# A two-layer hybrid decoder trunk: other buffer counts, joined attention scores, values in three chunks, a re-arranged end

## The chip, the cores and the metric

The kernel runs on one core of a Trainium2 chip. The metric is the device time of one execution in microseconds, as the median of several runs. The core has a matrix engine (TensorE, PE in the profile; PEld is its weight load), three engines for elementwise work (VectorE, DVE; ScalarE, ACT; GpSimd, POOL), and queues that start DMA transfers, most of them on SyncE (SP). Matmul results land in PSUM, which has eight banks of 512 float32 per partition; all else lives in SBUF.

## The reference

256 tokens of width 1024 go through two layers in float32. Cut to what matters:

```
x += 0.5 * SwiGLU_1(rms(x))                      # D_FF = 2816
h  = rms(x) @ W_in -> [rx | rgate | q | k | v | f_logit | gA | gB]
ya = (RG_LRU(conv4(rx)) * gelu(rgate)) @ w_rnn_out
# 8 heads of 128: q, k RMS-normalised
s  = q k^T / sqrt(128) + dcum[query] - dcum[key]   # dcum = cumsum(log_sigmoid(f_logit + f_b))
yb = (softmax(causal s) v) @ w_attn_out            # in query blocks of 128
x += (sigmoid(gA) * ya + sigmoid(gB) * yb) @ W_o
x += 0.5 * SwiGLU_2(rms(x))
x += sigmoid(rms(x) @ W_pg + b_pg) * (p @ W_pe)
# after both layers: final RMSNorm, output (1, 256, 1024)
```

## The kernel before

Activations stand transposed (features on partitions, tokens along the row) nearly everywhere. Every float32 factor is split into a high part, rounded to the matmul's own float32 format, and a low remainder, and a product is three matmuls: high by high, high by low, low by high (`mm3`, `mm3m`, L306 to L314; `mm2`, L344, does the first two as one 512-column matmul against the activation's high and low halves side by side).

**Weights** (`Weights`, L49 to L116) stream through SBUF in the order of a plan (L159 to L174). One entry of the plan is one DMA, mostly 1 MB, into a *raw* buffer (tag `wr`, three of them). It is cut into two *units*; of each, ScalarE writes the high part (L95) and VectorE the remainder (L96), into unit buffers (tags `wh` and `wl`, five of each). `next` (L110) hands a unit to the matmuls and emits the work for those up to four ahead. A raw buffer comes free when its second unit is split, a unit buffer when the matmuls that read it are done. `apart` (L98) loads one more 1 MB piece through a raw buffer into buffers of its own: the recurrent gates' weights in the first feed-forward's down projection of each layer, the embedding's in that of the second, both behind output tile 2 (L502). The down projection (L486 to L503) takes four units for each of its eight output tiles; an output tile's first matmul is that of L347.

**At the start**, four tiles `hd` hold input and first weights together (L181 to L189). They use the tag `wr` too, so that the fourth waits until the first has been used. `load_first` (L62) then loads the next two entries of the plan.

**Values** (L582 to L608): values and forget logits, 1032 columns, come in four chunks of 258. A chunk has two units of four 128-row blocks each, and for each of two token tiles and eight blocks three matmuls of 258 columns. `gates` (recurrent gates) follow the second, third and fourth chunk.

**Attention** goes head by head in four steps, spread over slots between the matmuls of other projections (`attend`, L753). `step_a` (L690) transposes q and k, splits them and makes a tile `b` (L705) that adds the forget terms in `step_b`. `step_b` (L707) makes the scores of query block 0 against 128 keys (four matmuls of 128 columns) and of block 1 against 256 keys (four of 256 columns) in one PSUM bank, and then for each block minimum (signs are turned), exponential and row sum, and scales the probabilities by the reciprocal on VectorE (L724). `step_c` (L728) transposes them on TensorE (L732), `step_d` multiplies by the values.

**The end** (L915 to L995): the last layer's gate product is made with tokens on partitions. Token tile 1's second half of the features is made in two halves of 256 columns (L990), both in one bank. `finish` (L939) reads the bank (L943), applies tanh (L944), forms the output (L945, L947), squares and sums it (L949) and multiplies by the final gain (L950). `scaled` (L952) forms the mean square (L955, L957), its power -1/2 on GpSimd (L959), and scales: 512 columns on ScalarE (L963), 512 on VectorE (L965), each followed by its output DMA (L966).

The order of instructions on each engine's queue is not the program's own: a planner that simulates the engines at build time sets it from the dependences, and inserts the waits. A dependence on a PSUM tile counts for the tile as a whole.

Of the kernel before, what the change touches and what calls it, by code (L numbers as in the profile page):

```python
# [16 lines left out]
P = 128  # L17
DEPTH = 2
D = 1024
# [21 lines left out]
VC = 258  # L41
# [78 lines left out]
def trunk(ctx: ExitStack, tc: tile.TileContext, head, xT, pT, vec, w1i, w1o, wf, wqk, wv, wg, wro, wao, wo, w2i, w2o,  # L120
# [85 lines left out]
    acol = cp.tile([P, NH], F32, name="acol")  # L206
    mcol = cp.tile([P, NH], F32, name="mcol")
    grp = cp.tile([P, 4], F32, name="grp")
    sel = cp.tile([P, 3], F32, name="sel")
# [27 lines left out]
    def constants():  # L237
        G.memset(mask, 0.0)
        G.affine_select(out=mask[:, P:], in_=mask[:, P:], pattern=[[-1, P]], compare_op=ALU.is_ge, fill=BIG,
                        base=0, channel_multiplier=1)  # L240
        trif = work(s="trif")
        G.memset(trif, 1.0)
        G.affine_select(out=trif[:, :P], in_=trif[:, :P], pattern=[[1, P]], compare_op=ALU.is_ge, fill=0.0,
                        base=0, channel_multiplier=-1)
        G.memset(lfh.bitcast(F32), 0.0)
        G.memset(lfl.bitcast(F32), 0.0)
        for t in rxp:
            G.memset(t[:, 0:3], 0.0)
        V.tensor_copy(out=tri, in_=trif)
        yield  # L250
        V.tensor_tensor(out=acol, in0=ident[:, 0:NH], in1=ident[:, 32:32 + NH], op=ALU.add)
        V.tensor_tensor(out=mcol, in0=ident[:, 64:64 + NH], in1=ident[:, 96:96 + NH], op=ALU.add)
        V.tensor_scalar(out=mcol, in0=mcol, scalar1=-1.0, scalar2=None, op0=ALU.mult)
        yield
        for g in range(4):
            V.tensor_reduce(out=grp[:, g:g + 1], in_=ident[:, 32 * g:32 * g + 32], axis=AX.X, op=ALU.add)
        yield
        V.tensor_tensor(out=sel[:, 0:1], in0=grp[:, 1:2], in1=grp[:, 3:4], op=ALU.add)
        V.tensor_scalar(out=sel[:, 0:1], in0=sel[:, 0:1], scalar1=-1.0, scalar2=None, op0=ALU.mult)
        V.tensor_tensor(out=sel[:, 1:2], in0=grp[:, 0:1], in1=grp[:, 1:2], op=ALU.add)  # L260
        V.tensor_tensor(out=sel[:, 2:3], in0=grp[:, 2:3], in1=grp[:, 3:4], op=ALU.add)
# [244 lines left out]
    def mix(l, n, wgp):  # L506
# [74 lines left out]

        Vh = big([P, TT, 4 * VC], F32R, "vh")  # L582
        Vl = big([P, TT, 4 * VC], F32R, "vl")
        z = kp.tile([P, TT * NH], F32, name=nm("z"), tag="z", bufs=1)
        for c in range(4):
            banks = [two[t]("v") for t in range(TT)]
            for w in range(2):
                wh, wl = W.next()
                for t in range(TT):
                    for i in range(4):  # L590
                        k = 4 * w + i
                        q = slice(i * VC, (i + 1) * VC)
                        mm3m(banks[t][:, 0:VC], a.hi(k, slice(t * P, (t + 1) * P)), a.lo(k, slice(t * P, (t + 1) * P)),
                             wh[:, q], wl[:, q], k == 0, k == KT - 1)
                if w == 0:
                    tick(2)
            for t in range(TT):
# [5 lines left out]
                if c == 3:  # L603
# [7 lines left out]
        dc = kp.tile([P, S], F32R, name=nm("dc"), tag="dc", bufs=1)  # L611
        dk = kp.tile([P, S], F32R, name=nm("dk"), tag="dk", bufs=1)

        def forget():
# [4 lines left out]
            for t in range(TT):  # L619
                oh = lfh[:, t].rearrange("p (g c) -> p g c", g=4)[:, :, 0:NH]  # L620
                ol = lfl[:, t].rearrange("p (g c) -> p g c", g=4)[:, :, 0:NH]
                V.tensor_copy(out=oh, in_=lf3[:, t].to_broadcast([P, 4, NH]))
                V.tensor_tensor(out=ol, in0=lf3[:, t].to_broadcast([P, 4, NH]), in1=oh.bitcast(F32), op=ALU.subtract)
# [9 lines left out]
            V.scalar_tensor_tensor(out=dc, in0=dh.bitcast(F32), scalar=sel[:, 0:1], in1=dps[:, 0:S], op0=ALU.mult,  # L633
                                   op1=ALU.add)
            V.tensor_scalar(out=dk, in0=dc.bitcast(F32), scalar1=sel[:, 1:2], scalar2=sel[:, 2:3], op0=ALU.mult,
                            op1=ALU.add)
# [53 lines left out]
        def step_a(h):  # L690
# [6 lines left out]
            s["q"] = qh, ql = awork(S, "aq", 5), awork(S, "aq", 5)  # L697
            s["k"] = kh, kl = awork(S, "aq", 5), awork(S, "aq", 5)
            s["b"] = awork(S, "aq", 5)
# [5 lines left out]
            A.activation(out=s["b"], in_=dc.bitcast(F32), func=AF.Identity, scale=mcol[:, h:h + 1], bias=acol[:, h:h + 1])  # L705

        def step_b(h):  # L707
            s = st[h]
            (qh, ql), (kh, kl), bl = s["q"], s["k"], s["b"]
# [7 lines left out]
            for t, o, nk in ((0, 0, P), (1, P, S)):  # L717
                V.tensor_tensor_reduce(out=sv[:, o:o + nk], in0=ps[:, o:o + nk], in1=mask[:, S - nk:S], scale=1.0,
# [220 lines left out]
    def finish(t, c, ps, pj, i):  # L939
# [10 lines left out]
        V.tensor_tensor(out=o, in0=o, in1=fgb[:, c], op=ALU.mult)  # L950

    def scaled(t, prior, i):  # L952
# [6 lines left out]
        G.tensor_tensor(out=r, in0=ms, in1=mhalf[:, 0:1], op=ALU.pow)  # L959
        for hf in range(2):  # L960
            o = xo[t][:, hf * 512:(hf + 1) * 512]
            if hf == 0:
                A.activation(out=o, in_=o, func=AF.Copy, scale=r)  # L963
            else:
                V.tensor_scalar(out=o, in0=o, scalar1=r, scalar2=None, op0=ALU.mult)  # L965
# [14 lines left out]
    for t in range(TT):  # L980
        finish(t, slice(0, 512), gp[t], pj[t], t)
    ws = [W.next() for _ in range(4)]
# [4 lines left out]
    pj[1], gp[1] = proj(1, 1), mmbank("gp")  # L987
    finish(0, slice(512, D), gp[0], pj[0], 2)
    scaled(0, [0], 2)
    for i in range(2):  # L990
        c = slice(i * S, (i + 1) * S)
        for u in range(4):
            gate(gp[1][:, c], 1, ws[u], u, c)
        finish(1, slice(512 + c.start, 512 + c.stop), gp[1][:, c], pj[1][:, c], 3 + i)
    scaled(1, [1, 3], 4)  # L995


def _layout(inputs):
# [22 lines left out]
    wv = vf.reshape(L, KT, P, 4, VC).transpose(0, 3, 2, 1, 4).reshape(L, 4, P, KT * VC)  # L1021
# [64 lines left out]
```

## Time and profile before

| | before |
|---|---|
| median of 3 runs, us (lowest to highest) | 1322.03 (1321.92 to 1322.12) |
| profiled execution, us: its time / its span | 1322.07 / 1320.4 |
| mean granted TensorE clock | 0.998 |
| PE busy, us (share of the span), instructions | 1309.2 (99%), 8504 |
| DVE busy | 1072.7 (81%), 2126 |
| ACT busy | 812.8 (62%), 1467 |
| DMA, mean share of 16 engines in the weights' queue | 51.3% |

The busy time of an engine is the union of its instructions' spans. Matmuls are pipelined, so their spans overlap, and what one costs is read from the distance between the starts of two.

### The profile page before, as it was taken

Reading aid. Unit: us, or ns where it says so; the run is one execution under the profiler, and the core shown is the slowest. Engines: PE = TensorE matmul, PEld = TensorE weight load, DVE = VectorE, ACT = ScalarE, POOL = GpSimd, SP = SyncE. Lnnn points to the kernel's source line nnn. Section 1 sums busy time; section 2 is a strip of 40 time slices with the busy share of each in tenths; the row PEclk is TensorE's granted clock in tenths of the full one; section 3 lists DMA queues with packets and bytes.
Section 4 is the critical chain, followed back from the end, with each engine's and each line's share of the span. In section 5 each row is a group of like instructions: output and inputs, shape, how many; then the busy total and the mean of one; then the engine's idle time right before and its main releaser. Section 6 shows DMA issues by size and latency. Waiting matters only on the chain.

```text
span 1320.4 us, 22211 instructions
## 1 busy us (share of the span) xinstructions
PE 1309.2 (99%) x8504; PEld 1191.2 (90%) x8504; DVE 1072.7 (81%) x2126; ACT 812.8 (62%) x1467; POOL 34.4 (3%) x44
## 2 busy tenths in 40 slices
PE   9999999999999999999999999999999999999997
PEld 8888899889999888889988888998899998888896
DVE  7998769899758899876789887698997678998765
ACT  6665656868655666555556656478676556655643
POOL 1000000020000000000000000000200000000000
PEclk9999999999999999999999999999999999999999
DMA  8654665444435555456445546644453455554660
GB/s 294 239 183 157 214 226 193 155 166 172 155 128 191 190 193 191 163 169 243 179 172 192 191 142 219 232 175 160 179 181 128 159 185 198 185 186 155 208 225 33
DMA packets 37258, 241.24 MB, mean 183 GB/s; under 512 B 4128, under 2 KB 4256, under 8 KB 14368
## 3 DMA queue, kind: packets, MB, share of 16 engines
q1 hardware_dynamic: 36864, 239.30, 51.3%
q8 instruction: 67, 1.10, 0.3%
q10 hardware_dynamic: 288, 0.52, 0.1%
q14 instruction: 39, 0.32, 0.1%
HBM read 238.76 MB, written 1.05 MB: 182 GB/s over the span
## 4 chain that ended last, share of the span: by engine, by line
PE 98%; DVE 0%; DMA 0%; ACT 0%; SPq 0%; issue 0%; POOLq 0%
PE mm L350 20%; PE mm L348 11%; PE at L350 11%; PE at L348 6%; PE f L307 3%; PE f L309 3%; PE f L308 3%; PE qk L312 2%; PE qk L314 2%; PE qk L313 2%; PE mm L309 2%; PE mm L307 2%; PE mm L308 2%; PE ya L350 2%; PE mm L347 2%; PE at L347 2%
## 5 line engine op out<-in xcount | busy, mean ns | idle before, releaser
L96 DVE TENSOR_TENSOR wl<-wr,wh 128x1024 fp32r<-128x1024 f32 (+2 forms) x476 | 538.9, 1135 | 147.0 <-ACT wh L95 141.6
L95 ACT ACTIVATE wh<-wr 128x1024 fp32r<-128x1024 f32 (+2 forms) x476 | 467.4, 986 | 307.7 <-PE mm L350 88.3
L350 PE MATMUL mm<-h,wh 128*128 128x512 f32 x616 | 219.3, 394 | 0.0
L350 PE MATMUL at<-h,wh 128*128 128x512 f32 x616 | 218.5, 394 | 0.0
L348 PE MATMUL mm<-h,wl 128*128 128x256 f32 x704 | 182.4, 281 | 0.0
L348 PE MATMUL at<-h,wl 128*128 128x256 f32 x704 | 181.7, 281 | 0.5 <-DVE wl L96 0.5
L350 PE MATMUL mm<-f,wh 128*128 128x512 f32 x504 | 176.8, 394 | 0.0
L348 PE MATMUL mm<-f,wl 128*128 128x256 f32 x528 | 144.1, 280 | 0.0
L348 PEld LDWEIGHTS at<-h,wl 128*128 128x128 f32 x704 | 131.8, 188 | 9.0 <-DVE wl L96 1.0
L348 PEld LDWEIGHTS mm<-h,wl 128*128 128x128 f32 x704 | 131.9, 188 | 7.8 <-DVE wl L96 0.4
L350 PEld LDWEIGHTS mm<-h,wh 128*128 128x128 f32 x616 | 115.7, 188 | 22.5
L350 PEld LDWEIGHTS at<-h,wh 128*128 128x128 f32 x616 | 115.0, 188 | 21.9
L350 PEld LDWEIGHTS mm<-f,wh 128*128 128x128 f32 x504 | 94.5, 188 | 20.7
L307 PE MATMUL f<-h,wh 128*128 128x256 f32 x384 | 108.6, 283 | 0.0
L309 PE MATMUL f<-h,wl 128*128 128x256 f32 x384 | 108.5, 282 | 0.0
L308 PE MATMUL f<-h,wh 128*128 128x256 f32 x384 | 108.4, 282 | 0.0
L348 PEld LDWEIGHTS mm<-f,wl 128*128 128x128 f32 x528 | 99.4, 188 | 2.1
L308 PEld LDWEIGHTS f<-h,wh 128*128 128x128 f32 x384 | 72.4, 189 | 0.1
L307 PEld LDWEIGHTS f<-h,wh 128*128 128x128 f32 x384 | 72.4, 188 | 0.1
L309 PEld LDWEIGHTS f<-h,wl 128*128 128x128 f32 x384 | 72.4, 189 | 0.0
L384 ACT ACTIVATE sum<-mm 128x256 f32<-128x256 f32 x112 | 40.0, 375 | 49.2 <-PE mm L350 49.1
L385 DVE TENSOR_TENSOR sum<-mm,sum 128x256 f32<-128x256 f32 x112 | 45.1, 420 | 14.3 <-ACT sum L384 14.3
(305 smaller groups left out, 2818.0 us busy)
## 6 DMA issues: line engine op xcount, KB each, us to landing
wr<-in_w2i SPq DMA_DIRECT2D x44, 1024.0 KB, 4.8
wr<-in_w1i SPq DMA_DIRECT2D x41, 1024.0 KB, 4.8
wr<-in_wf SPq DMA_DIRECT2D x32, 1024.0 KB, 4.8
wr<-in_w1o SPq DMA_DIRECT2D x32, 704.0 KB, 4.0
wr<-in_w2o SPq DMA_DIRECT2D x32, 704.0 KB, 4.0
wr<-in_wqk SPq DMA_DIRECT2D x16, 1024.0 KB, 4.8
wr<-in_wv SPq DMA_DIRECT2D x8, 1032.0 KB, 5.0
wr<-in_wro SPq DMA_DIRECT2D x8, 1024.0 KB, 4.8
```

The source lines that it names most:

```text
L95: self.nc.scalar.activation(out=hi[:, c], in_=src[:, c], func=AF.Copy)
L96: self.nc.vector.tensor_tensor(out=lo[:, c], in0=src[:, c], in1=hi[:, c].bitcast(F32), op=ALU.subtract)
L307: T.matmul(ps, lhsT=wh, rhs=xh, start=first, stop=False)
L308: T.matmul(ps, lhsT=wh, rhs=xl, start=False, stop=False)
L309: T.matmul(ps, lhsT=wl, rhs=xh, start=False, stop=last)
L312: T.matmul(ps, lhsT=xh, rhs=wh, start=first, stop=False)
L313: T.matmul(ps, lhsT=xh, rhs=wl, start=False, stop=False)
L347: T.matmul(ps, lhsT=wh, rhs=t, start=True, stop=False, skip_group_check=True)
L348: T.matmul(ps[:, 0:S], lhsT=wl, rhs=t[:, 0:S], start=False, stop=False, skip_group_check=True)
L350: T.matmul(ps, lhsT=wh, rhs=t, start=False, stop=last, skip_group_check=True)
L384: A.activation(out=o, in_=ps[:, S:], func=AF.Copy)
L385: V.tensor_tensor(out=o, in0=ps[:, 0:S], in1=o, op=ALU.add)
```

## The change

Raw buffers go from three to two and unit buffers from five to six; the four tiles of the start move to the pool `big`. Values come in three chunks of 344 columns, and a unit of them holds three blocks in place of four; the gates follow the first, second and third chunk. `step_a` makes no tile `b`; k's high and low part stand in one tile. `step_b` makes the scores of both query blocks with six matmuls: three of 256 columns for block 1, one of 256 columns for block 0 against high and low keys at once, one of 128, and one of 384 that adds the forget terms of both from `dk`; its weights are one column of the constant `pick`, repeated 128 times. The low-key part of block 0 is added with the mask into `m0`. The probabilities are scaled on ScalarE. At the end, each half of the last gate product gets a bank of its own, the gain multiply stands in a function `gained` that is called behind the start of the power, and the scaling of the first 512 columns is divided between ScalarE and VectorE. The rest (constants, layout of the weights in memory) follows from these.

```diff
-VC = 258
+NV3 = 3
+VC = 344
-        plan += [(wv[l, c], [4 * VC, 4 * VC]) for c in range(4)]
+        plan += [(wv[l, c], [3 * VC, 3 * VC]) for c in range(4)]
-    W = Weights(nc, wp, plan, ahead=4, raw_bufs=3, unit_bufs=5, big=big)
+    W = Weights(nc, wp, plan, ahead=4, raw_bufs=2, unit_bufs=6, big=big)
-        t = wp.tile([P, 2, HC], F32, name=f"hd{i}", tag="wr", bufs=W.raw_bufs)
+        t = big([P, 2, HC], F32, f"hd{i}")
...
-        for c in range(4):
+        for c in range(NV3):
             banks = [two[t]("v") for t in range(TT)]
-            for w in range(2):
-                wh, wl = W.next()
+            for k in range(KT):
+                i = (KT * c + k) % 3
+                if i == 0:
+                    wh, wl = W.next()
+                q = slice(i * VC, (i + 1) * VC)
                 for t in range(TT):
...
-            for g in ([], [0, 1], [2, 3], [4])[c]:
+            for g in ([0, 1], [2, 3], [4])[c]:
                 gates(g)
...
-            A.activation(out=s["b"], in_=dc.bitcast(F32), func=AF.Identity, scale=mcol[:, h:h + 1], bias=acol[:, h:h + 1])
...
             ps = atbank("s")
-            for t, o, nk in ((0, 0, P), (1, P, S)):
-                q = slice(t * P, (t + 1) * P)
-                mm3(ps[:, o:o + nk], qh[:, q], ql[:, q], kh[:, 0:nk], kl[:, 0:nk], True, False)
-                T.matmul(ps[:, o:o + nk], lhsT=bl[:, q], rhs=dk[:, 0:nk], start=False, stop=True)
+
+            def mm(o, w, r, start=False, stop=False):
+                T.matmul(ps[:, o], lhsT=w, rhs=r, start=start, stop=stop, skip_group_check=True)
+            mm(slice(0, S), qh[:, q1], kk[:, 1], start=True)
+            mm(slice(0, S), qh[:, q1], kk[:, 0])
+            mm(slice(0, S), ql[:, q1], kk[:, 0])
+            mm(slice(S, 2 * S), qh[:, q0], kk[:, :, q0])
+            mm(slice(S, S + P), ql[:, q0], kk[:, 0, q0])
+            mm(slice(0, S + P), pick[:, h:h + 1].to_broadcast([P, P]), dk, stop=True)
...
+            m0 = work(s="m0")
+            V.tensor_tensor(out=m0[:, q0], in0=ps[:, S + P:], in1=mask[:, q1], op=ALU.add)
...
-                V.tensor_scalar(out=pr[:, o:o + nk], in0=pr[:, o:o + nk], scalar1=rs[:, t:t + 1], scalar2=None,
-                                op0=ALU.mult)
+                A.activation(out=pr[:, o:o + nk], in_=pr[:, o:o + nk], func=AF.Copy, scale=rs[:, t:t + 1])
...
-        V.tensor_tensor(out=o, in0=o, in1=fgb[:, c], op=ALU.mult)
-
-    def scaled(t, prior, i):
+
+    def gained(t, c):
+        V.tensor_tensor(out=xo[t][:, c], in0=xo[t][:, c], in1=fgb[:, c], op=ALU.mult)
+
+    def scaled(t, prior, i, rest):
...
+        p = G.tensor_tensor(out=r, in0=ms, in1=mhalf[:, 0:1], op=ALU.pow)
+        gained(t, rest)
         for hf in range(2):
             o = xo[t][:, hf * 512:(hf + 1) * 512]
...
+            for q in range(2):
+                s = o[:, q * S:(q + 1) * S]
+                if hf == 0 and q == 0:
+                    A.activation(out=s, in_=s, func=AF.Copy, scale=r)
+                elif q == 1 and hf == 0:
+                    V.tensor_scalar(out=s, in0=s, scalar1=r, scalar2=None, op0=ALU.mult)
+                elif q == 0:
+                    V.tensor_scalar(out=o, in0=o, scalar1=r, scalar2=None, op0=ALU.mult)
...
     for i in range(2):
         c = slice(i * S, (i + 1) * S)
+        f = slice(512 + c.start, 512 + c.stop)
+        ps = mmbank("gp")[:, c]
         for u in range(4):
-            gate(gp[1][:, c], 1, ws[u], u, c)
-        finish(1, slice(512 + c.start, 512 + c.stop), gp[1][:, c], pj[1][:, c], 3 + i)
-    scaled(1, [1, 3], 4)
+            gate(ps, 1, ws[u], u, c)
+        finish(1, f, ps, pj[1][:, c], 3 + i)
+        if i == 0:
+            gained(1, f)
+    scaled(1, [1, 3], 4, f)
```

## Rows read from the trace of the kernel before

**Rows 1.** The page's part 4: shares of the chain that ended last, by engine.

```profile
PE 98%; DVE 0%; DMA 0%; ACT 0%; SPq 0%; issue 0%; POOLq 0%
```

**Rows 2.** TensorE's waits in the whole execution: us in total, times, longest.

```profile
PE warm L874 <- POOL ones L192: 1.1, 1, 1.1
PE gp L312 <- DVE s L955: 0.7, 1, 0.7
PE at L348 <- DVE wl L96: 0.5, 2, 0.3
```

**Rows 3.** Timeline of TensorE, 308 to 315 us: start, us, engine, line, operation.

```profile
308.50 0.22 PE L308 MATMUL s<-aq,aq 128*128 128x128 f32 x1
308.56 0.27 PE L309 MATMUL s<-aq,aq 128*128 128x128 f32 x1
308.67 0.28 PE L714 MATMUL s<-dk,aq 128*128 128x128 f32 x1
...
309.33 0.28 PE L309 MATMUL f<-h,wl 128*128 128x256 f32 x1
...
314.99 0.29 PE L309 MATMUL f<-h,wl 128*128 128x256 f32 x1
```

**Rows 4.** Timeline of TensorE, gate product near the end.

```profile
1285.32 0.40 PE L314 MATMUL gp<-wh,h 128*128 128x512 f32 x1
...
1291.59 0.39 PE L314 MATMUL gp<-wh,h 128*128 128x512 f32 x1
```

**Rows 5.** Timeline of TensorE, second value chunk of layer 0 and what follows.

```profile
221.20 0.28 PE L313 MATMUL v<-wl,h 128*128 128x258 f32 x1
...
226.84 0.28 PE L307 MATMUL g<-xch,wbh 128*128 128x256 f32 x1
```

**Rows 6.** Timeline, head 0 of layer 0: scaling on VectorE, first transpose on TensorE.

```profile
300.62 0.54 DVE L724 TENSOR_SCALAR pr<-pr,rs 128x128 f32<-128x128 f32 x2
...
302.02 0.27 PE L732 MATMUL pt<-ident,pr 128*128 128x128 f32 x1
```

**Rows 7.** Timeline of TensorE, VectorE, ScalarE, the end.

```profile
1307.88 0.28 PE L314 MATMUL gp<-wh,h 128*128 128x256 f32 x1
...
1308.84 0.39 PE L312 MATMUL gp<-wh,h 128*128 128x256 f32 x1 [0.67 <-DVE s L955]
...
1311.65 0.28 PE L314 MATMUL gp<-wh,h 128*128 128x256 f32 x1
1311.97 0.48 DVE L943 SCALAR_TENSOR_TENSOR z<-gp,R,pbb 128x256 f32<-128x256 f32 x1 [0.51 <-PE gp L314]
...
1314.38 0.43 DVE L950 TENSOR_TENSOR xo<-xo,fgb 128x256 f32<-128x256 f32 x1 [0.57 <-ACT z L949]
1314.73 0.15 DVE L957 SCALAR_TENSOR_TENSOR s<-ss,s 128x1 f32<-128x1 f32 x1
...
1315.61 0.72 ACT L963 ACTIVATE xo<-xo,s 128x512 f32<-128x512 f32 x1 [1.26 <-POOL s L959]
1315.61 0.49 DVE L965 TENSOR_SCALAR xo<-xo,s 128x512 f32<-128x512 f32 x1 [0.73 <-POOL s L959]
1316.36 0.34 ACTq L966 DMA_DIRECT2D out_dram<-xo  x1
```

**Rows 8.** Timeline, down projection of layer 0, tiles 2 to 4; last line: page, DMA issues.

```profile
148.71 0.83 DVE L96 TENSOR_TENSOR wl<-wr,wh 128x640 fp32r<-128x640 f32 x1
...
150.80 2.01 ACT L95 ACTIVATE wbh<-wra 128x1024 fp32r<-128x1024 f32 x2 [0.27 <-DMA wra<-in_wg]
...
153.99 0.85 ACT L95 ACTIVATE wh<-wr 128x768 fp32r<-128x768 f32 x1
...
154.17 0.82 DVE L96 TENSOR_TENSOR wl<-wr,wh 128x640 fp32r<-128x640 f32 x1
...
160.96 0.39 PE L347 MATMUL mm<-f,wh 128*128 128x512 f32 x1
...
wr<-in_w1o SPq DMA_DIRECT2D x32, 704.0 KB, 4.0
```

More of the change, by code (lines that the diff above doesn't have):

```diff
@@ L204, in trunk @@
     tri = cp.tile([P, S], F32R, name="tri")
[L206 to L209, printed above, removed]
+    neglo = cp.tile([P, 1], F32, name="neglo")
+    pick = cp.tile([P, NH], F32R, name="pick")
     lfh = cp.tile([P, TT, P], F32R, name="lfh")
@@ L250, in constants @@
         yield
[L251 to L261, printed above, removed]
+        V.tensor_tensor(out=pick, in0=ident[:, 0:NH], in1=ident[:, 32:32 + NH], op=ALU.add)
+        V.tensor_reduce(out=neglo, in_=ident[:, 32:64], axis=AX.X, op=ALU.add)
+        V.tensor_scalar(out=neglo, in0=neglo, scalar1=-1.0, scalar2=None, op0=ALU.mult)
         yield
@@ L579, in scan @@
             V.tensor_tensor_scan(out=xc[:, m], data0=at[:, m], data1=tq[:, m], initial=0.0, op0=ALU.mult, op1=ALU.add)
-        Vh = big([P, TT, 4 * VC], F32R, "vh")
-        Vl = big([P, TT, 4 * VC], F32R, "vl")
+        Vh = big([P, TT, NV3 * VC], F32R, "vh")
+        Vl = big([P, TT, NV3 * VC], F32R, "vl")
         z = kp.tile([P, TT * NH], F32, name=nm("z"), tag="z", bufs=1)
-        for c in range(4):
+        for c in range(NV3):
             banks = [two[t]("v") for t in range(TT)]
-            for w in range(2):
-                wh, wl = W.next()
-                for t in range(TT):
[L590 to L595, printed above, removed]
+            for k in range(KT):
[3 more added lines that the diff above has]
+                q = slice(i * VC, (i + 1) * VC)
+                for t in range(TT):
+                    mm3m(banks[t][:, 0:VC], a.hi(k, slice(t * P, (t + 1) * P)), a.lo(k, slice(t * P, (t + 1) * P)),
+                         wh[:, q], wl[:, q], k == 0, k == KT - 1)
+                if k in (2, 5):
                     tick(2)
@@ L602, in mix @@
                                        op0=ALU.mult, op1=ALU.subtract)
-                if c == 3:
+                if c == NV3 - 1:
                     V.scalar_tensor_tensor(out=z[:, t * NH:(t + 1) * NH], in0=banks[t][:, VC - NH:VC], scalar=r,
                                            in1=vt[:, l, VEC["fb"]:VEC["fb"] + NH], op0=ALU.mult, op1=ALU.add)
-            for g in ([], [0, 1], [2, 3], [4])[c]:
+            for g in ([0, 1], [2, 3], [4])[c]:
                 gates(g)
             tick(2)
-        dc = kp.tile([P, S], F32R, name=nm("dc"), tag="dc", bufs=1)
-        dk = kp.tile([P, S], F32R, name=nm("dk"), tag="dk", bufs=1)
+        dk = kp.tile([P, S + P], F32R, name=nm("dk"), tag="dk", bufs=1)
         def forget():
@@ L619, in forget @@
             for t in range(TT):
[L620 to L623, printed above, removed]
+                oh = lfh[:, t].rearrange("p (g c) -> p g c", g=4)[:, 0:2, 0:NH]
+                ol = lfl[:, t].rearrange("p (g c) -> p g c", g=4)[:, 0:2, 0:NH]
+                V.tensor_copy(out=oh, in_=lf3[:, t].to_broadcast([P, 2, NH]))
+                V.tensor_tensor(out=ol, in0=lf3[:, t].to_broadcast([P, 2, NH]), in1=oh.bitcast(F32), op=ALU.subtract)
             yield
@@ L632, in forget @@
             A.activation(out=dh, in_=dps[:, 0:S], func=AF.Copy)
[L633 to L636, printed above, removed]
+            for o, n_ in ((0, S), (S, P)):
+                V.scalar_tensor_tensor(out=dk[:, o:o + n_], in0=dh[:, 0:n_].bitcast(F32), scalar=neglo,
+                                       in1=dps[:, 0:n_], op0=ALU.mult, op1=ALU.add)
         qk = [None, None]
@@ L696, in step_a @@
                     T.transpose(ps[:, (w * TT + t) * P:(w * TT + t + 1) * P], qk[cb][:, w, t, hh * P:(hh + 1) * P], ident)
-            s["q"] = qh, ql = awork(S, "aq", 5), awork(S, "aq", 5)
-            s["k"] = kh, kl = awork(S, "aq", 5), awork(S, "aq", 5)
-            s["b"] = awork(S, "aq", 5)
+            s["q"] = qh, ql = awork(S, "aq", 2), awork(S, "aq", 2)
+            s["k"] = kk = kp.tile([P, 2, S], F32R, name=nm("ak"), tag="ak", bufs=1)
+            kh, kl = kk[:, 0], kk[:, 1]
             g = gqk[:, l:l + 1]
@@ L704, in step_a @@
             V.scalar_tensor_tensor(out=kl, in0=ps[:, S:], scalar=g, in1=kh.bitcast(F32), op0=ALU.mult, op1=ALU.subtract)
-            A.activation(out=s["b"], in_=dc.bitcast(F32), func=AF.Identity, scale=mcol[:, h:h + 1], bias=acol[:, h:h + 1])
         def step_b(h):
             s = st[h]
-            (qh, ql), (kh, kl), bl = s["q"], s["k"], s["b"]
+            (qh, ql), kk = s["q"], s["k"]
+            q0, q1 = slice(0, P), slice(P, S)
             ps = atbank("s")
-            for t, o, nk in ((0, 0, P), (1, P, S)):
-                q = slice(t * P, (t + 1) * P)
-                mm3(ps[:, o:o + nk], qh[:, q], ql[:, q], kh[:, 0:nk], kl[:, 0:nk], True, False)
-                T.matmul(ps[:, o:o + nk], lhsT=bl[:, q], rhs=dk[:, 0:nk], start=False, stop=True)
+            def mm(o, w, r, start=False, stop=False):
[6 more added lines that the diff above has]
+            mm(slice(0, S + P), pick[:, h:h + 1].to_broadcast([P, P]), dk, stop=True)
             sv = pr = awork(384, "pr", 2, F32)
             mx, rs = small(TT, "mx", "sa"), small(TT, "rs", "sa")
-            for t, o, nk in ((0, 0, P), (1, P, S)):
-                V.tensor_tensor_reduce(out=sv[:, o:o + nk], in0=ps[:, o:o + nk], in1=mask[:, S - nk:S], scale=1.0,
+            m0 = work(s="m0")
+            V.tensor_tensor(out=m0[:, q0], in0=ps[:, S + P:], in1=mask[:, q1], op=ALU.add)
+            for t, o, nk, pc, mk in ((0, 0, P, slice(S, S + P), m0[:, q0]), (1, P, S, slice(0, S), mask)):
+                V.tensor_tensor_reduce(out=sv[:, o:o + nk], in0=ps[:, pc], in1=mk, scale=1.0,
                                        scalar=3e38, op0=ALU.add, op1=ALU.min, accum_out=mx[:, t:t + 1])
@@ L981, in trunk @@
         finish(t, slice(0, 512), gp[t], pj[t], t)
+        gained(t, slice(0, 512))
     ws = [W.next() for _ in range(4)]
@@ L1020, in _layout @@
     vf = np.concatenate([v, f], axis=2)
-    wv = vf.reshape(L, KT, P, 4, VC).transpose(0, 3, 2, 1, 4).reshape(L, 4, P, KT * VC)
+    wv = vf.reshape(L, KT, P, NV3, VC).transpose(0, 3, 1, 2, 4).reshape(L, 4, 6, P, VC)
+    wv = wv.transpose(0, 1, 3, 2, 4).reshape(L, 4, P, 6 * VC)
     wg = np.zeros((L, P, KT, 2, P), np.float32)
```

9 lines of the change are left out of this document (2 added, 7 removed).

## The prediction

> **What bounds the kernel now.** Three views, in this order. First the chain that ended last: the reader is to see that TensorE alone carries 98% of it [rows 1], so only two kinds of edit can pay, those that take time out of TensorE's own stream, and those in the stretch behind its last matmul. Second, TensorE's waits: in the whole execution they come to less than 3 us: 1.1 us before its very first instruction, 0.5 us (and another 0.4) at the start for the split of the first weights, and 0.7 us near the end [rows 2]. No weight load and no attention step makes TensorE wait inside, so nothing that only frees VectorE, ScalarE or the DMA queue can show, except by preventing a wait that isn't there. Third, the timeline, for the pitch, the time from the start of one matmul to that of the next. The busy column overlaps (a 256-column matmul shows 0.28 us), so the pitch is the price. From 309.33 to 314.99 it is 5.66 us over 48 matmuls of 256 columns, 0.118 us [rows 3]; from 1285.32 to 1291.59 it is 6.27 us over 27 of 512 columns, 0.232 us [rows 4]; from 221.20 to 226.84 it is 5.64 us over 47 of 258 columns, 0.120 us [rows 5]. Between 256 and 512 columns that is a slope of 0.446 ns a column over a constant of about 4 ns. At 128 columns it stops falling: a 128-column matmul whose successor is another of 128 takes 0.11 us (308.56 to 308.67), and 0.06 us where the row before had run longer (308.50 to 308.56) [rows 3]. Each matmul here has its own weight load, and a short matmul can't cover the next one's.
>
> The profiled execution took 1322.07 us, of which 1320.4 is the span; the median of the runs is 1322.03, 0.04 below. The sum is made against the former.
>
> **The values in three chunks.** Each layer's 192 matmuls of 258 columns become 144 of 344: the same 49,536 columns, 48 matmuls fewer. By the line through 256 and 512 columns, 344 cost 0.118 + 88 x 0.446 ns = 0.157 us. Before: 192 x 0.120 = 23.04 us; after: 144 x 0.157 = 22.65 us; 0.4 us a layer, 0.8 in both. 258 columns lie 1.1 ns above that line; if 344 do too, it is 22.81 and 0.5 for both. I take 0.6. The gate matmuls that are moved one chunk forward stay in the same TensorE stream and cost the same there.
>
> [...]
>
> **The joined scores.** Per head, eight matmuls (four of 128 columns for the first query block, four of 256 for the second) become six: four of 256, one of 128, one of 384; 1536 columns in both. Before, seven stand from 308.50 to 309.33, 0.83 us, and the eighth, issued earlier among other matmuls, is taken at 0.06: 0.89 [rows 3]. After: 4 x 0.118, the 128 at 0.11 because a short one is followed by a weight load, and 384 at 0.118 + 128 x 0.446 ns = 0.175: 0.76 us. That is 0.13 a head, 2.1 us for 16 heads, which I take. With the 128 at 0.06 it is 0.18 a head, 2.9 us. Two things no row shows: a moving operand in two separate pieces of 128, and a weight tile read from one repeated column. Bounded by two 128s in place of one 256 (0.22 for 0.118) and by one more short weight load (0.06), they would take 0.16 a head and leave a loss of 0.5 us. I stay by the plain pitches, since every other operand in that list has the shape of a row.
>
> **What lies beside TensorE.** One ScalarE operation a head goes, the two scalings (0.54 us on VectorE [rows 6]) move to ScalarE, VectorE gets a 128-column add, and the first block's softmax starts only when the common last matmul is done. The Copy-with-scale of 512 columns takes 0.72 us on ScalarE [rows 7], so 384 take no more; the add takes at most the 0.54 of the two scalings. The path from scores to the transposes of the probabilities then grows by at most 0.72 - 0.54 + 0.54 = 0.72 us. In head 0 of a layer, the tightest, VectorE ends the scaling at 301.16 and the transpose starts at 302.02, 0.86 us later [rows 6]. So I cost it at nothing; if that cover is gone, the transposes wait for the rest. What is queued behind the scalings on ScalarE is the next weight split, and TensorE works from units already split. The smaller constants and the forget edits lie beside TensorE too: nothing.
>
> **Weight buffers.** Look at the down projection where the extra gate weights are loaded. The last split for output tile 3 ends at 154.17 + 0.82 = 154.99, the first one for tile 4, from the next chunk, starts on ScalarE at 153.99, and TensorE first needs it at 160.96 [rows 8]. With two raw buffers that chunk's load can't be issued before 154.99; it lands 4.0 us later [rows 8], 159.0, and 0.85 on ScalarE and about as much on VectorE make it 160.8: no wait, but next to no slack if the order stays. The sixth unit buffer works the other way: a split need not wait for the unit five before it, so the 154.99 comes earlier, by up to the time that TensorE takes for one unit. I cost both together at nothing; the range keeps a loss. At the start, the first weights' tiles leave the raw buffers, so the fourth of them and the next loads are issued at once; the queue order is unchanged, and the early waits [rows 2] are for the first two tiles, which come no sooner. Nothing, and at most 0.5 us either way.
>
> **The end.** The second half of the last gate product starts at 1308.84, held 0.67 us by VectorE's read of the first half out of the same bank [rows 7]. With a bank of its own it starts one pitch after 1307.88, at 1308.00. Its 24 matmuls then need 23 pitches, 2.71 us, to the start of the last (before 2.81, to 1311.65 [rows 7]): 1310.71, 0.94 earlier. Next on the path is VectorE's gain multiply at 1314.38, behind which the sum of squares waits until 1314.73: moved under the power on GpSimd, it gives back 0.35. The final scaling would then start at 1315.61 - 1.29 = 1314.32. Of it, ScalarE's 0.72 [rows 7] shrinks to a quarter; late next is VectorE, which does a quarter of 256 columns (some 0.27, by 0.49 for 512) and then 512 (0.49): 1315.08, and the last output DMA is issued at 1315.10 in place of 1316.36. That is 1.26; I take 1.3. If a gain multiply of 0.43 stands in front of the critical read on VectorE once or twice, 0.4 to 0.8 is left; 1.6 if the other queue's output lands a little sooner.
>
> **Sum:** 0.6 + 2.1 + 1.3 = 4.0 us off 1322.07: 1318.07, against the median 1318.0.
>
> **Rivals.** *A, starved splits (slower).* Place: the down projections, each with an extra 1 MB load beside the main chunks, four in all. With two raw buffers that load can't go out before the split that ends at 148.71 + 0.83 = 149.54, whereas before its data was being split from 150.80 [rows 8]. Landing at least 4.0 us later, it is split from 153.5 on, 2.7 us later than before, 3 with its larger size. If the order on ScalarE keeps it ahead of tile 3's last split, that one, the next load and the next split all slip by about 3 us past the point without slack: 4 x 3 = 12 us, 1322.1 - 4.0 + 12 = 1330. The gain is eaten from 1.0 us a place on, and from 1.7 the kernel is measurably slower. For it: the order of before does put the extra split first (150.80, before 154.17). Against: one more unit buffer lets the other one go earlier.
>
> *B, the scores cost their columns.* The joined scores save nothing, the unseen operand forms eating the 0.13 us: 1322.0 - 0.6 - 1.3 = 1320.1. For it: the columns are the same. Against: the 0.11 us rows. [...]
>
> *C, the softmax is late.* ScalarE, held in front of a split that waits, delays the scalings, and the transposes wait some 0.2 us in each of 16 heads: 3.2 us, so 1318.0 + 3.2 = 1321.2. For it: only 0.86 us of slack in head 0. Against: the other heads have over 2 us between scaling and transpose (head by head along the timeline).
>
> **How the numbers follow.** Forecast 0.70, A 0.11, B 0.09, C 0.10. About 0.2%, 2.6 us, is what a measurement of this kernel can tell from no change. The forecast's own range is 1316.4 (2.9 + 0.8 + 1.6 with 0.3 of the start) to 1319.4. Below it and above it lie A, B and C; B and C end within 2.6 us of before, A beyond. To hold 8 in 10 the range takes in B and most of the forecast's upper bounds: 1316.0 to 1321.0, leaving out A and part of C. Faster 0.70, same 0.19, slower 0.11.
>
> **What would show it.** Right: 144 value matmuls a layer at 0.157 us; six score matmuls a head in about 0.76 us; no wait of TensorE in front of the second half, its last matmul some 0.94 us nearer to the first half; at most 1.1 us from the sum of squares to the final scaling; TensorE's waits still under 3 us. Wrong: a wait of TensorE on a split in a down projection (A), a score list that still takes 0.89 (B), waits of the transposes on ScalarE (C), or a gain multiply on VectorE in front of the last read.

## The result, and the profile after

| | before | after |
|---|---|---|
| median, us (lowest to highest) | 1322.07 (in the same runs) | 1336.41 (1334.58 to 1337.34) |
| ratio, 95% interval | | 1.0107 (1.0095 to 1.0119) |
| profiled execution, us: its time / its span | 1322.07 / 1320.4 | 1337.34 / 1335.6 |
| mean granted TensorE clock | 0.998 | 0.998 |
| PE busy, us, instructions | 1309.2, 8504 | 1311.9, 8376 |
| DVE busy / ACT busy, us | 1072.7 / 812.8 | 1064.8 / 809.8 |

The change made the kernel 14.3 us slower; 4 us faster had been forecast. TensorE has 128 instructions fewer, as foreseen, at the same clock, and VectorE and ScalarE are busy 7.9 and 3.0 us less (the union of TensorE's overlapping spans is 2.7 us longer, which says little about its work). So the time went into waits. The chain of waits says so first: TensorE carries 80% of it, not 98% [rows 1].

```profile
PE 80%; DVE 8%; DMA 7%; ACT 3%; issue 1%; POOL 1%; SPq 0%; POOLq 0%; ACTq 0%; DVEq 0%
```

TensorE's waits in the kernel after (us in total, times, longest), its first lines:

```profile
PE f L298 <- DVE g L759: 9.3, 10, 1.7
PE mm L298 <- ACT h L331: 1.5, 2, 0.9
PE warm L871 <- POOL ones L193: 1.1, 1, 1.1
...
PE pt L729 <- ACT pr L722: 0.6, 1, 0.6
```

The first line did not exist [rows 2]. `f` is a filler: one of 24 projections a layer that are laid between the attention steps. It needs a PSUM bank, and the bank is freed by `g`, VectorE's read of an earlier filler. Call a *gap* what the distance of two starts has above the median pitch of that number of columns, if it is more than 0.1 us. TensorE's whole stream has 4.4 us of gaps before and 23.1 after; 8.2 of these lie between 280 and 400 us and 7.4 between 940 and 1040, the attention stretches of the two layers, where there were none.

Values, layer 0, after (timeline of TensorE): 11 pitches in 1.73 us, 0.157 us [rows 5].

```profile
227.20 0.32 PE L304 MATMUL v<-wl,h 128*128 128x344 f32 x1
...
228.93 0.32 PE L303 MATMUL v<-wh,h 128*128 128x344 f32 x1
```

A head's scores and the wait behind them (timeline of TensorE, after) [rows 3]:

```profile
369.00 0.75 PE L704 MATMUL s<-ak,aq 128*128 128x256 f32 x5
369.59 0.39 PE L704 MATMUL s<-dk,pick 128*128 128x384 f32 x1
371.68 0.39 PE L298 MATMUL f<-h,wh 128*128 128x256 f32 x1 [1.70 <-DVE g L759]
```

The last matmuls of two fillers before that (timeline of TensorE, after):

```profile
357.88 0.28 PE L300 MATMUL f<-h,wl 128*128 128x256 f32 x1
...
364.64 0.28 PE L300 MATMUL f<-h,wl 128*128 128x256 f32 x1
```

VectorE in the same stretch. `m` is `m0`, the added operation, which needs these scores:

```profile
365.94 1.22 DVE L97 TENSOR_TENSOR wl<-wr,wh 128x1024 fp32r<-128x1024 f32 x1 [1.85 <-ACT wh L96]
...
367.88 0.47 DVE L693 SCALAR_TENSOR_TENSOR ak<-tr,gqk,ak 128x256 fp32r<-128x256 f32 x1
369.54 1.23 DVE L97 TENSOR_TENSOR wl<-wr,wh 128x1024 fp32r<-128x1024 f32 x1 [1.19 <-ACT wh L96]
370.68 0.42 DVE L329 TENSOR_TENSOR ot<-o,ot 128x256 fp32r<-128x256 f32 x1
371.01 0.28 DVE L714 TENSOR_TENSOR m<-s,mask 128x128 f32<-128x128 f32 x1
371.21 1.07 DVE L759 TENSOR_TENSOR g<-f,RB 128x256 f32<-128x256 f32 x3
```

The reader is to see the bunch `x3`: three banks are read one after another, directly behind `m0`, while TensorE has stood still for 1.70 us. The last matmuls of these three fillers had ended at 358.17, 361.52 and 364.92 us, 13.0 to 7.0 us before their `g`. Over the 48 fillers, the time from a filler's last matmul to its `g` reaches 14.9 us in the kernel after (about half are above 10) and 2.6 before. Idle time of VectorE (1.85 and 1.19 us here) was there to read them. The scores themselves end at 369.98; what is left of the wait is a weight split and a read of `o`, which also stand ahead of `m0`.

In these 3.04 us of idle time no `g` passes the `m0` ahead of it: the bunch starts at 371.21 us, behind `m0` at 371.01.

The start of head 0's transposes, after: ScalarE's scaling ends late enough to hold TensorE once, 0.64 us [rows 6].

```profile
302.18 0.79 ACT L722 ACTIVATE pr<-pr,rs 128x128 f32<-128x128 f32 x2
...
302.62 0.33 PE L729 MATMUL pt<-ident,pr 128*128 128x128 f32 x1 [0.64 <-ACT pr L722]
```

The end, after (timeline of TensorE, VectorE, GpSimd, the queues) [rows 7]:

```profile
1324.31 0.28 PE L305 MATMUL gp<-wh,h 128*128 128x256 f32 x1
...
1324.43 0.28 PE L303 MATMUL gp<-wh,h 128*128 128x256 f32 x1
...
1327.17 0.28 PE L305 MATMUL gp<-wh,h 128*128 128x256 f32 x1
...
1329.90 0.16 DVE L956 SCALAR_TENSOR_TENSOR s<-ss,s 128x1 f32<-128x1 f32 x1 [0.57 <-ACT z L946]
1329.97 0.42 DVE L949 TENSOR_TENSOR xo<-xo,fgb 128x256 f32<-128x256 f32 x1
1330.20 0.60 POOL L958 TENSOR_TENSOR s<-s,mhalf 128x1 f32<-128x1 f32 x1 [4.97 <-DVE s L956]
...
1331.62 0.34 SPq L970 DMA_DIRECT2D out_dram<-xo  x1
```

The second half starts one pitch behind the first, and from the first half's last matmul to the last output DMA it is 7.31 us instead of 8.48.

The extra gate weights of the first down projection (timeline of ScalarE, after) [rows 8] are split 3.0 us later than before, as rival A had it, but no matmul from 142 to 162 us waits (and no split makes TensorE wait in the other three down projections either):

```profile
153.80 2.01 ACT L96 ACTIVATE wbh<-wra 128x1024 fp32r<-128x1024 f32 x2 [2.98 <-DMA wra<-in_wg]
```

### The profile page after: what moved, and what is told of

It reads as the page before. It is cut to its first block, busy times and chain, and to the rows that moved or that the text cites. A ratio compares the mean times of both kernels' runs of the same rounds, so it can differ in the third digit from the quotient of the medians.

```text
span 1335.6 us, 21907 instructions
## 1 busy us (share of the span) xinstructions
PE 1311.9 (98%) x8376; PEld 1189.9 (89%) x8376; DVE 1064.8 (80%) x2100; ACT 809.8 (61%) x1479; POOL 37.1 (3%) x44
## 4 chain that ended last, share of the span: by engine, by line
PE 80%; DVE 8%; DMA 7%; ACT 3%; issue 1%; POOL 1%; SPq 0%; POOLq 0%; ACTq 0%; DVEq 0%
PE mm L341 15%; PE at L341 11%; PE mm L339 9%; PE at L339 6%; DVE wl L97 4%; PE f L298 3%; PE f L299 3%; PE f L300 3%; DMA wr<-in_wf 2%; ACT wh L96 2%; PE ya L341 2%; PE mm L338 2%; DMA wr<-in_w2o 2%; PE at L338 2%; PE o L341 1%; DMA wr<-in_w1o 1%
## 5 line engine op out<-in xcount | busy, mean ns | idle before, releaser
L96 ACT ACTIVATE wh<-wr 128x1024 fp32r<-128x1024 f32 (+2 forms) x476 | 462.4, 984 | 275.0 <-PE mm L341 37.9
```

The source lines that it names most:

```text
L96: self.nc.scalar.activation(out=hi[:, c], in_=src[:, c], func=AF.Copy)
```

## The experiments

Each ratio is to the kernel before, with its 95% interval. Theory 1 lays the loss on the weight buffers, its rivals on the attention steps.

**Parts undone, one at a time.** The kernel after with the old buffers:

```diff
-raw_bufs=2, unit_bufs=6
+raw_bufs=3, unit_bufs=5     # and hd back in tag wr
```

> The changed kernel with three raw and five unit buffers again, all else as changed. Theory 1 (the buffers: with two raw and six unit buffers the splits of weights stand earlier in the queues of ScalarE and VectorE, wait there, and hold up the drains of the projections' PSUM banks behind them): the waits of TensorE in the attention stretch go, 1318 to 1319 us. Theory 2 (the scores: the added mask operation and the scaling on ScalarE make the drains late): 1334 to 1337, as the changed kernel. Theory 3 (only both together): 1318 to 1319, as theory 1.

Measured: 1336.14 us, 1.0109 (1.0092 to 1.0126), and 11.4 us of waits of `f` for `g`. Theory 1 falls as the main cause; theory 2 has the time.

The buffers alone, in the kernel before:

```diff
-raw_bufs=3, unit_bufs=5
+raw_bufs=2, unit_bufs=6     # and hd in pool big
```

> The kernel before with two raw and six unit buffers (and the start's tiles in the other pool), nothing else changed. Theory 1: the same waits of some 18 us appear, 1337 to 1341 us. Theories 2 and 3: no wait, 1321 to 1323.

Measured: 1327.58 us, 1.0041 (1.0026 to 1.0056). No expectation had this: the buffers cost 5.5 us, and undoing them in the kernel after gave nothing back, since there other waits took their place.

The scaling back on VectorE, in the kernel after:

```diff
-A.activation(out=pr[...], in_=pr[...], func=AF.Copy, scale=rs[:, t:t + 1])
+V.tensor_scalar(out=pr[...], in0=pr[...], scalar1=rs[:, t:t + 1], op0=ALU.mult)
```

> The changed kernel with the scaling of the probabilities on VectorE again. Theory 1: no difference beyond 2 us, 1334 to 1339. Theory 2: if the scalings on ScalarE are what is late, the waits go, 1318 to 1322; if the mask operation is, 1330 to 1337.

Measured: 1344.54 us, 1.0169 (1.0154 to 1.0185), above every range, with 13.1 us of waits of `f` for `g`. The scaling on ScalarE is a help, not the cause.

The kernel after with the old score step (`step_a`, `step_b` and their constants as before, scaling on VectorE too):

> The changed kernel with the score step of before (eight matmuls a head, tile b, scaling on VectorE), and the buffers, values and end as changed. Theory 1: waits stay, scores cost 1.9 us more: 1336 to 1340. Theories 2 and 3: waits go, 1319 to 1321.

Measured: 1324.05 us, 1.0017 (1.0008 to 1.0026); waits of `f` for `g` 0.9 us. That is 3 us above what theories 2 and 3 had, but the large loss is gone: it belongs to the joined scores.

**The buffer of m0.** `m0` comes from `work`, a ring of 12 buffers under one tag; `g` comes from it as well. The idea of theory 4: buffers of one ring are handed out in program order while the queues' order is being set. A `g` that comes behind `m0` in the program can then not be set ahead of it in VectorE's queue, however early its matmuls end, and `m0` waits for the scores. In the kernel after, with a buffer of its own:

```diff
-m0 = work(s="m0")
+m0 = awork(S, "m0", 2, F32)
```

> The changed kernel with one edit: the masked low-key scores m0 get buffers of their own, not one of the 12 of 256 columns (tag w) that the projections' drains g use too. Theory 4 (shared buffers: they are handed out in the program's order, so on VectorE every drain g that comes behind m0 in the program also stands behind it in the queue, and m0 waits for the scores): the drains follow their projections within 4 us again, TensorE's waits on g go, and what is left over the forecast's 1318 is the buffers' 5.5 us: 1322 to 1325 us. Theory 5 (the added operation and the later softmax themselves, whatever buffer): 1334 to 1338, no change.

Measured: 1328.84 us, 1.0050 (1.0036 to 1.0063); `f` waits 0.8 us for `g`. The wait goes as theory 4 has it; the time is 4 us above its range. The same with the old weight buffers:

> As y1_own_m0, and three raw and five unit buffers again. Theory 4: both causes are gone, the three terms of the forecast are left (values 0.7, scores 1.9, end 1.2): 1317.5 to 1319.5. Theory 5: 1334 to 1338, as x1_buffers_back.

Measured: 1324.10 us, 1.0014 (1.0006 to 1.0023). The waits for `g` are gone, but the time is 6 us above the forecast, and 5 above theory 4's range.

The order in the traces shows the rule. In the program 0, 1, 3, 6, 8, 11, 13 and 16 fillers of a layer stand ahead of the `m0` of heads 0 to 7. In the kernel after, VectorE has done exactly 0, 1, 3, 6, 8, 11, 13 and 16 `g` when these `m0` start, in both layers; with `m0` in a buffer of its own (1324.10) it has done 1, 6, 9, 14, 16, 20, 22 and 24. A ring that was merely short of buffers would not give the program's order to the unit.

Then the same operation put alone into the kernel before, once from the shared ring and once from a buffer of its own:

```diff
+m0 = work(s="m0")                  # second run: awork(P, "m0", 1, F32)
+V.tensor_tensor(out=m0[:, 0:P], in0=src, in1=mk, op=ALU.add)
```

> The kernel before with one operation more a head: the first block's scores are masked on VectorE into a tile m0 of the shared 12 buffers, and the minimum is taken from there; the same values come out. Theory 4: the drains queue up behind m0, 1330 to 1338. Theory 5: 16 operations of 0.29 us beside TensorE, 1322 to 1325, and no difference to b2_add_own_tag.

> As b1_add_shared_tag, but m0 in a buffer of its own. Theory 4: the drains stay where they were, 1321.5 to 1323.5. Theory 5: as b1_add_shared_tag, within 2 us of it.

Measured: 1341.55 us, 1.0149 (1.0135 to 1.0163), with the ring; 1324.86, 1.0022 (1.0013 to 1.0032), with its own. Both lie above theory 4's ranges, by 3.6 and 1.4 us, but theory 5's "no difference" is out: two kernels with the same instructions differ by 16.7 us through the buffer that one tile takes. With the ring the `g` stand in the program's order again, 0, 1, 3, 6, 8, 11, 13, 16. A larger ring was not run. TensorE's waits, ring first:

```profile
PE f L307 <- DVE g L767: 14.0, 8, 1.9
```

```profile
PE warm L879 <- POOL ones L192: 1.1, 1, 1.1
PE pt L737 <- DVE pr L729: 0.9, 2, 0.5
```

**Which buffer count costs 5.5 us.** The buffers alone, but with five unit buffers:

```diff
-raw_bufs=2, unit_bufs=6
+raw_bufs=2, unit_bufs=5
```

> The kernel before with two raw weight buffers and the head's buffers of their own, but five unit buffers. The three edits on buffers together cost 5.5 us. Theory R (two raw buffers: a load and so a split waits until the pair before is split, and VectorE and ScalarE do the splits at worse times): 1326 to 1329, the cost is all there. Theory U (six unit buffers let splits be placed ahead of drains): 1321.5 to 1323.

Measured: 1322.97 us, 1.0006 (0.9997 to 1.0015). So 4.6 of the 5.5 us come with the sixth unit buffer. ScalarE near 195 us shows how, six buffers first, then five:

```profile
189.80 2.00 ACT L95 ACTIVATE wh<-wr 128x1024 fp32r<-128x1024 f32 x2
195.46 2.01 ACT L95 ACTIVATE wh<-wr 128x1024 fp32r<-128x1024 f32 x2 [3.66 <-DMA wr<-in_wf]
197.37 0.49 ACT L340 ACTIVATE h<-x,vt 128x256 fp32r<-128x256 f32 x1
```

```profile
193.21 0.51 ACT L340 ACTIVATE h<-x,vt 128x256 fp32r<-128x256 f32 x1 [1.81 <-DVE x L499]
193.62 0.40 ACT L401 ACTIVATE sq<-x 128x256 f32<-128x256 f32 x1
194.23 1.06 ACT L95 ACTIVATE wh<-wr 128x1024 fp32r<-128x1024 f32 x1 [0.20 <-DMA wr<-in_wf]
```

With a sixth buffer two splits are set ahead of the activation `h`; ScalarE stands idle for 3.66 us until their DMA has landed, and `h`, which TensorE needs next, stands behind them. TensorE then waits near 197, 297, 638, 671, 852 and 952 us, 0.5 to 1.1 us each, 4.7 in all. Near 638 and 852 us the picture is the same (ScalarE idle for 2.58 and 4.15 us in front of two splits, then `h`). Near 297 and 952 `f` waits for a `g` that stands behind weight splits on VectorE; the wait near 671 was not explained. Whether a sixth unit buffer would do this with three raw ones was not tried.

**What is left with m0's own buffer.** As 1324.10, with the scaling on VectorE:

> As the run with m0's own buffer and 3 raw and 5 unit weight buffers (1324.10), with the probabilities scaled on VectorE instead of ScalarE. There TensorE waited 2.4 us for a weight split of ScalarE near 385 and 1038 us. If scaling on ScalarE makes that split late: the waits go, 1320.5 to 1322.0. If the added m0 in the last head's chain is the cause, TensorE waits there for the probabilities instead (0.6 + 0.3 us a layer in the run with the added operation alone): 1322.0 to 1323.5. If neither, 1323.5 to 1324.7.

Measured: 1326.66 us, 1.0035 (1.0021 to 1.0048): worse by 2.6, so none of the three; why was not followed. Without `m0`: the low-key part goes into the same columns by a 128-column matmul of its own (old buffers, scaling on VectorE):

```diff
-mm(slice(S, 2 * S), qh[:, q0], kk[:, :, q0])
+mm(slice(S, S + P), qh[:, q0], kk[:, 1, q0])
+mm(slice(S, S + P), qh[:, q0], kk[:, 0, q0])
```

> The whole change with 3 raw and 5 unit buffers, the probabilities scaled on VectorE, and the second term of the first half's scores added in the bank by a 128-column matmul (two of 128 in place of one of 256), so that the added VectorE operation m0 is gone. Theory 5 (the added operation, by its buffer and by its place in the chain of the last head, is all that eats the joined scores' gain): 1322.07 - 0.7 - 1.9 - 1.2 = 1318.3, 1318.0 to 1319.9 with up to 0.1 us for each of 16 added matmuls, and no wait over 0.5 us in the attention stretches. Rival 6 (a bank of joined scores is readable only after its last matmul, so the softmax of the last head is late whatever VectorE does): 1321 to 1322.5, with waits of TensorE near 385 and 1038 us.

Measured: 1320.25 us, 0.9987 (0.9978 to 0.9996), no wait over 0.6 us but that before the first instruction, and no gap in the attention stretches. So the waits go with `m0`, and rival 6 is out; the time is 0.35 us above theory 5's range. With the 128-column matmuls between the 256-column ones:

> As the joined scores without m0 (1320.25), but the three 128-column matmuls each stand between the 256-column ones. In the trace of that run a 128-column matmul behind another 128-column one took 0.109 us, in the changed kernel one behind a 256-column matmul 0.060 us. Theory 5 (only m0 ate the gain): the scores cost 16 x (3 x 0.120 + 3 x 0.060 + 0.229) = 12.3 us instead of 15.3 before, and the time is 1320.25 less 1.6 to 2.6, 1317.5 to 1318.7, without a wait in the attention stretches. Rival: the pitch of 0.060 needs the 256-column matmul on both sides only by chance and the time stays at 1319.8 to 1320.5.

Measured: 1320.20 us, 0.9986 (0.9977 to 0.9995): the rival. A 128-column matmul behind one of 256 does take 0.060 us, but the 256-column one behind it takes 0.171 instead of 0.120. The pair costs 0.231 us, as much as 0.109 and 0.120 by themselves.

The scaling on ScalarE added to that:

> The same with the probabilities scaled on ScalarE, so all of the change but the buffers and m0. If the scaling on ScalarE costs nothing where there is cover (as predicted): within 0.7 us of the interleaved run on VectorE. If its two instructions of 0.4 us behind Exp make a weight split late in the last head, 1.0 to 2.5 us more, with a wait of TensorE for ScalarE's wh near 385 and 1038 us.

Measured: 1319.35 us (1319.09 to 1319.74), 0.9979 (0.9970 to 0.9987): 0.85 less, a little more than expected, and no wait near 385 or 1038 us. This is the fastest version run, all of the change but `m0` and the weight buffers. Its chain and waits:

```profile
PE 99%; DMA 0%; DVE 0%; ACT 0%; SPq 0%; POOLq 0%; issue 0%; DVEq 0%
```

```profile
PE warm L870 <- POOL ones L193: 1.1, 1, 1.1
PE at L338 <- ACT wh L96: 0.6, 1, 0.6
PE at L339 <- DVE wl L97: 0.3, 1, 0.3
```

Its VectorE reads each filler by itself, two of the three here in the moment when the matmul `f` ends:

```profile
362.75 0.42 DVE L758 TENSOR_TENSOR g<-f,RB 128x256 f32<-128x256 f32 x1 [0.79 <-PE f L300]
...
366.27 0.42 DVE L758 TENSOR_TENSOR g<-f,RB 128x256 f32<-128x256 f32 x1 [0.62 <-PE f L300]
...
369.88 0.43 DVE L758 TENSOR_TENSOR g<-f,RB 128x256 f32<-128x256 f32 x1
```

And with the weight buffers of the change, so the whole change without `m0`:

> The whole change, weight buffers too, with only m0 removed in this way. Theory 4 and U together: m0 is the large cause and the sixth unit buffer the small one, and they add: the run without buffers plus 4.6 us, 1322 to 1324. If the sixth buffer costs only where VectorE's queue is loaded by other work, and m0 was that work, 1317.5 to 1319.5. If m0 was not the large cause, 1330 or more.

Measured: 1323.14 us, 1.0009 (1.0000 to 1.0019). The buffers cost 3.8 us here, and the shared `m0` makes the rest, 1336.41 - 1323.14 = 13.3 (with the score matmul that it saves a head already taken off): 5.7 with a buffer of its own (1328.84) and 7.6 more from the ring. The steps don't add in every order: with the old weight buffers `m0` costs 4.8 by itself and the ring 12.0 more (1319.35, 1324.10, 1336.14).

**Time or place.** As 1324.10, with the wide half's softmax first and `m0` behind it:

```diff
-for t, o, nk, pc, mk in ((0, 0, P, ...), (1, P, S, ...)):
+for t, o, nk, pc, mk in ((1, P, S, ...), (0, 0, P, ...)):   # m0 made at t == 0
```

> As the run with m0's own buffer, 3 raw and 5 unit buffers and scaling on ScalarE (1324.10), with the second half of the scores (256 wide, without m0) handled first, so that its Exp starts before m0. If what is left there is m0's 0.28 us ahead of the whole softmax, Exp of the wide half starts about 0.5 us sooner and the last heads' waits of 3.7 us shrink by 0.5 to 1.5 us: 1322.5 to 1323.6. If it is the order of splits around the softmax that the added instruction shifts, any time from 1321 to 1326 and the waits move to other places.

Measured: 1322.59 us, 1.0007 (0.9998 to 1.0017): 1.5 less, but not where it was expected. In the two traces, whose executions differ by only 0.7 us (1323.16 and 1322.45), the gaps around the last heads are 4.2 us in both, and the first 10 us of the kernel make the difference. `m0` only in heads 0 to 6, the last head as in the interleaved run:

```diff
+joint = h < 7        # second run: h % 2 == 1
```

> The interleaved run with scaling on ScalarE (1319.35), but heads 0 to 6 of each layer with the joined 256-column matmul and m0 in a buffer of its own; the last head without m0. In the runs with m0 in a buffer of its own the last head's scores start at 381 to 384 us, without m0 at 372 to 376 us, and TensorE's waits of 3.5 to 5.7 us stand near the end of the stretches. Theory P (place: m0 in the heads before makes the planner set the last head later, where no filler is left behind its softmax): the waits of about 4 us stay although this head has no m0, 1322.3 to 1324. Theory O (the operation in the last head's own chain): the waits go and the matmuls saved in 14 heads show, 1317.9 to 1319.3.

> The same with m0 in the odd heads only, the last among them. In the planned order the last head's scores stand 290 matmuls ahead of the merge, where it is 312 without m0 (1319.35, no waits) and 256 with m0 in all heads (waits of 3.5 us). Theory P: the cover suffices for most of it, waits of at most 1 us, and 8 heads save 0.07 us each: 1318.7 to 1320. Theory O: the last head has m0, so the waits of 3.5 to 4 us are there: 1322 to 1323.5.

Measured: 1324.52 us, 1.0016 (1.0006 to 1.0025), and 1320.25, 0.9986 (0.9977 to 0.9994). Both are theory P's, 0.5 and 0.25 us above its ranges: the place decides. In the first, the last head has no `m0` and yet waits as before: its scores start at 381.18 us, against 372.15 in the fastest version. ScalarE and then TensorE of the first:

```profile
383.91 0.49 ACT L727 ACTIVATE pr<-pr,mx 128x256 f32<-128x256 f32 x1
384.31 0.19 ACT L727 ACTIVATION_READ_ACCUMULATOR pr<-pr,mx 128x1 f32 x1
384.95 1.06 ACT L96 ACTIVATE wh<-wr 128x1024 fp32r<-128x1024 f32 x1 [0.45 <-ACT pr L727]
```

```profile
381.18 0.85 PE L704 MATMUL s<-ak,aq 128*128 128x256 f32 x6
...
384.47 0.39 PE L341 MATMUL ya<-yr,wh 128*128 128x512 f32 x1
386.06 0.50 PE L338 MATMUL ya<-yr,wh 128*128 128x512 f32 x1 [1.20 <-ACT wh L96]
```

Here the fillers are over. A weight split stands behind this head's exponentials, and TensorE needs it at once; the gaps there are 2.1 us in layer 0. In the second, the last head has `m0`, starts at 375.50, and the gaps there are 0.7 us a layer. Why the planner sets the last head later when earlier heads have `m0` is not shown.

**Values and end alone.** The kernel before with the parts "values" and "end" of the change:

> The kernel before with the three value chunks and the new end alone; buffers and scores as before. If the parts add (measured in the changed kernel's trace: values 46.0 to 45.3 us, end about 1.2 us earlier) it takes 1322.07 - 0.7 - 1.2 = about 1320.1, 1319.7 to 1320.6. If every part also shifts other work into new waits, as the others did, 1321.5 or more.

Measured: 1320.32 us, 0.9987 (0.9978 to 0.9996), as the sum of the two terms has it.

## Why the prediction was wrong

**Right: the three terms.** The values gave 46.0 - 45.3 = 0.7 us (forecast 0.6), the joined scores 15.3 - 13.4 = 1.9 (2.1), the end 8.48 - 7.31 = 1.2 (1.3): 3.8 us, forecast 4.0. The end's term was made up as forecast: the second half starts one pitch behind the first, and the values and the end alone gave the sum of their terms. The bounds for operand forms that no row showed weren't needed: of the 16 matmuls with a moving operand in two pieces 12 have the plain pitch (0.118 to 0.121 us; the other four, behind a matmul with a pitch of 0.03, have 0.200 to 0.203), and the weight load from a repeated column lasts 0.19 us as the others do. The 384-column matmul takes 0.229 us where 0.175 was expected, the 128-column one before it 0.060 where 0.11 was: the same sum, with part of the short one's cost showing at the next matmul.

**Wrong: "What lies beside TensorE ... So I cost it at nothing".** This step priced the added VectorE operation by its duration and by head 0's 0.86 us of slack. That part was nearly right: one wait of 0.64 us. It did not ask which buffer the operation takes, and what then has to stand behind it in VectorE's queue. The operation waits for the scores; the 24 reads a layer that free TensorE's banks come from the same ring and were set in the program's order, so behind it: 7.6 us here, 12.0 with the old weight buffers, 16.7 in the kernel before. And with a buffer of its own the operation still moves the planned order: the last head of layer 0 starts 6.6 us later in the kernel before (381.08 against 374.50) and 9.8 in the change with the old weight buffers (381.95 against 372.15), out of its cover, with gaps of 2.6 and 4.2 us there, both layers together. That is most of the 2.8 and 4.8 us by which these kernels are slower than those without `m0`. The prediction's own rule, to name what is queued behind a waiting instruction, was applied to the scalings on ScalarE and not to `m0` on VectorE.

**Wrong: "I cost both together at nothing" (weight buffers).** They cost 3.8 us in the change without `m0` and 5.5 in the kernel before, 4.6 of these with the sixth unit buffer. The step looked at the down projections, where nothing waited, and took a sixth buffer as pure freedom. Freedom for the splits was what cost: they were set ahead of work that TensorE needs.

**The rivals.** A (starved splits, 1330) came nearest in time and was wrong in place: the gate weights were 3.0 us later, as it worked out, and nothing waited. B (columns alone) was wrong for six matmuls a head; with seven it nearly came out, 15.3 to 14.7 us in the fastest version. C (late softmax) described the kind of wait that remains in the last heads with `m0` in a buffer of its own, but on another cause. That the change would push a reader of PSUM back in a queue stood in no case: the 0.11 for slower was given to A alone.

**What the fastest version lacks to the forecast:** 1319.35 against 1318.0. Of the scores' 2.1 us only 15.3 - 14.7 = 0.6 came, so 1.5 is missing there; the other terms gave as much as forecast.

## What to carry to other kernels

Of an added operation, ask three things: how long it takes, for what it waits, and which buffers it shares with work that must not wait for that; where the order is set from a ring of buffers, the last can cost more than the other two (16.7 us against 2.8 here). A deeper buffer on one stream lets that stream be set earlier, also ahead of work on the critical path (4.6 us with the sixth unit buffer here); look for queue entries that wait for a DMA with a needed operation behind them. When a part is taken out to test it, do it also in the kernel before: in the kernel after, the buffers' cost was hidden by the larger wait.

## What the runs showed of the hardware

A matmul of 128 columns in 0.060 us is not a gain by itself: the matmul behind it takes longer (0.171 in place of 0.120 for 256 columns; 0.229 for 384, where the line through 256 and 512 has 0.175), and a pair of 128 and 256 columns, each with its own weights, costs about 0.23 us whether the two are mixed or each stands behind its like. The weight loads keep a distance too. Those of the last two 128-column matmuls of rows 3 and of the two 256-column ones behind them start 0.11 us apart (timeline of TensorE's weight loads, before):

```profile
308.50 0.19 PEld L309 LDWEIGHTS s<-aq,aq 128*128 128x128 f32 x1
308.61 0.19 PEld L714 LDWEIGHTS s<-dk,aq 128*128 128x128 f32 x1
308.72 0.19 PEld L307 LDWEIGHTS s<-aq,aq 128*128 128x128 f32 x1
308.83 0.19 PEld L308 LDWEIGHTS s<-aq,aq 128*128 128x128 f32 x1
```

Of the 8503 distances between the starts of two weight loads in that trace, 15 are below 0.10 us. That such a distance makes both the 0.11 us of a 128-column matmul behind its like and the longer pitch of its successor is an estimate from these figures; no run tested it by itself.

Scaling 128 and then 256 columns takes 0.79 us for both on ScalarE and 0.54 on VectorE [rows 6], and yet moving it to ScalarE saved 0.85 us in the version without waits in the attention stretches, 2.6 with `m0` in a buffer of its own and 8.1 in the changed kernel. Why it saves was not shown.
